# A two-block transformer on one core: conditioning steps spread anew over the feed-forward layers, and projections that end tile by tile

## The chip, the core and the metric

The kernel runs on one core of a Trainium2 chip. The core has a matrix engine (PE, with its weight loads PEld), a vector engine (DVE), a scalar engine (ACT), a general engine (POOL) and a sync engine (SP), which here does nothing but issue loads; 16 DMA engines move the data. The metric is the device time of one execution in microseconds (us).

## What is computed

All is float32. A first block of two layers works on 256 tokens of 1024 features, a second block of four layers on these and on 256 context tokens. What the change touches lies in the first block, and in the conditioning rows `sh`, `sc`, `gt`, which need only `c` and `c_ctx` and can be computed at any time before the second block.

```python
def conv_ffn(h, w_up, ffn_dw_w, ffn_dw_b, w_down):
    u = causal_dwconv(h @ w_up, ffn_dw_w, ffn_dw_b)
    gate, val = jnp.split(u, 2, axis=-1)
    return (jax.nn.silu(gate) * val) @ w_down
...
# first block, each layer l; token_mix ends with "return merged @ w_o"
mix = token_mix(h, positions, w_in[l], ..., w_o[l])
h = layer_norm(DEEPNORM_ALPHA * h + mix, ln1_g[l], ln1_b[l])
ffn = conv_ffn(h, w_up[l], ffn_dw_w[l], ffn_dw_b[l], w_down[l])
h = layer_norm(DEEPNORM_ALPHA * h + ffn, ln2_g[l], ln2_b[l])
...
# second block, each layer i
sh, sc, gt = jnp.split(jax.nn.silu(c) @ ada_w[i] + ada_b[i], 3, axis=-1)
shc, scc, gtc = jnp.split(jax.nn.silu(c_ctx) @ ada_w[i] + ada_b[i], 3, axis=-1)
h = rms_norm(x, norm_g[i]) * (1.0 + sc[:, None]) + sh[:, None]
```

`w_o` is 1024 x 1024, `w_up` 1024 x 5632, `w_down` 2816 x 1024, `ada_w` four times 1024 x 3072.

## The kernel before

**Weights.** All weights lie packed in one array in the order in which they are read (`_plan`), cut into loads of 512 KB. `wload` (L167) issues the next load on SP's queue into a tile `raw` (pool `raw`, 3 buffers, or the side pool `raw2`, 5 buffers). A load waits for the instruction that last read its buffer, and the queue is worked in order. `wsplit` (L177) makes two tiles of a raw one: `whi`, a rounded copy by ACT (L185), and `wlo`, the remainder by DVE (L186). `mm3` (L199) adds three matmuls for each product: hi by lo, hi by hi, lo by hi. `chunk` (L189) loads and splits a whole chunk at high priority: the scheduler, which writes each engine's order, puts it ahead of other work.

**A first-block layer** is `token_mix`, `proj_ln`, `ffn`. `proj_ln` (L731) multiplies by `w_o` in four chunks of 256 columns; each has two token tiles t of 128, and each tile's sum is added to the residual `x[t]` (L744) with statistics per chunk (L745). `layer_norm` (L340) then makes mean and 1/sqrt of each tile (`rsqrt`, some 11 small DVE instructions), scales both halves of 512 features (L352, L353), and `to_feat` (L232) transposes them on PE (L237), copies them on ACT (L238) and subtracts on DVE (L239). The result `hT` is what the next matmuls need.

**The feed-forward part** (`ffn`, L753) takes 22 steps f. Each has an up chunk of 256 columns (two loads, 48 matmuls of 256 columns), a short convolution and gate on ACT and DVE, and, two steps later, the down products of that f: one load of `w_down`, 12 matmuls of 512 columns into four accumulators (`down`). At the end comes the second norm (L811, L812, `layer_norm`).

**Conditioning.** The rows take 96 steps, 48 in each layer. A step (`ada_step`, L277) is one load of 512 KB into `raw2` and four matmuls 32 x 256 (L291, counted in the profile as eight instructions). Eight steps fill one accumulator `ps_o`, which DVE then adds to the bias (L295) and POOL writes to a tensor `adar`. Table `ADA_F` sets five steps ahead of step f = 0, 38 within the feed-forward steps (one or two each) and five behind the last.

**Tiles of pool `big`** (4 buffers, 16 KB in each partition) hold `hT`, the combined branches, the gates and `mT`, the input of `w_o`.

In the words below, "x0" and "x1" are the two token tiles, and T0 is the start of the first up matmul of f = 0.

Of the kernel before, what the change touches and what calls it, by code (L numbers as in the profile page):

```python
# [73 lines left out]
def _plan():  # L74
# [3 lines left out]
    ada = [(i, w, k) for i in range(4) for w in range(3) for k in range(KT)]  # L78
    for l in range(2):
# [16 lines left out]
        for j in range(4):  # L96
            p.chunk("w_o", l, a(256 * j, 256 * j + 256))
# [40 lines left out]
class _Net:  # L138
    def __init__(self, ctx, tc, io, out, dbg):
# [17 lines left out]
        self.load = 0  # L157
        self.ada_acc = None
# [6 lines left out]
    # weights  # L165

    def wload(self, side=False):  # L167
# [3 lines left out]
        t = (self.raw2 if side else self.raw).tile([128, RAWN], F32, name="raw")  # L171
        w = self.io["ws"]
        self.nc.sync.dma_start(t[:, :n], bass.AP(tensor=w.tensor, offset=w.offset + self.off, ap=[[n, 128], [1, n]]))
# [3 lines left out]
    def wsplit(self, src, n, side):  # L177
        nc = self.nc
        pool = self.wsp2 if side else self.wsp
# [9 lines left out]
    def chunk(self, n_k=KT, side=False):  # L189
        """The next chunk: [(hi, lo)] per row tile of 128, each [128, columns]."""  # L190
        out = []
        with self.tc.high_priority() if self.load >= 4 else ExitStack():
            while len(out) < n_k:
                t, k, c = self.wload(side)
                hi, lo = self.wsplit(t, k * c, side)
                out += [(hi[:, b * c:(b + 1) * c], lo[:, b * c:(b + 1) * c]) for b in range(k)]
        return out

# [33 lines left out]
    def to_feat(self, src, hi_dst, lo_dst):  # L232
        """Transposes src [128 tokens, 512] to 4 tiles of features, split in hi and lo."""
# [7 lines left out]
    def qstack(self, ps, n, pool, name="qs", bufs=2):  # L241
        """ps: [two heads x 64, n]; returns [128, head, n] with hi and lo of a head stacked."""
# [8 lines left out]
    def kstack(self, ps, n, hh, ll):  # L251
        """hh: hi of a head on both halves, [128, head, n]; ll: lo on the half of the head, zeros on the other."""
# [8 lines left out]
    def logits(self, out, qs, e, qsl, ks, ksl):  # L261
        """q . k of head e: hi.lo, then (hi + lo).hi."""
# [14 lines left out]
    def ada_step(self):  # L277
        nc = self.nc
        if not self.ada_todo:
            return  # L280
        i, w, k = self.ada_todo.pop(0)
        with self.tc.high_priority():
            t, _, _ = self.wload(True)
# [9 lines left out]
        if k == KT - 1:  # L293
            row = self.w1.tile([128, 256], F32, name="adarow")
            nc.vector.tensor_tensor(row, ps[:, :256], self.ada_b, op=OP.add)  # L295
# [7 lines left out]
    # set-up  # L303

    def setup(self):
# [10 lines left out]
        # the first norm's gains and offsets, spread over the partitions by the tensor engine  # L316
# [44 lines left out]
    def block1(self):  # L361
        nc, tc = self.nc, self.tc
        with ExitStack() as ctx:
# [13 lines left out]
            for l in range(2):  # L377
# [4 lines left out]
                hT = self.proj_ln(l, m)  # L382
                with ExitStack() as c2:
# [4 lines left out]
                    hT = self.ffn(l, hT)  # L388
# [59 lines left out]
    def rope1(self, z, H, t):  # L448
        """In place on z [128, H * 64]."""
# [11 lines left out]
    def token_mix(self, l, hT):  # L461
# [46 lines left out]
        # scores and the chosen keys  # L508
# [32 lines left out]
        # attention over the chosen keys  # L541
# [50 lines left out]
    def conv_in(self, l, hT):  # L592
# [3 lines left out]
        w = self.chunk()  # L596
# [15 lines left out]
        # pooling  # L612
# [8 lines left out]
    def conv_pool(self, l, comb):  # L621
# [27 lines left out]
        # depthwise convolution, its layer norm and silu  # L649
# [609 lines left out]
```

## Time and profile before

| | us |
|---|---|
| median of 3 runs | 2018.33 (2016.28 to 2025.07) |
| span of the profiled execution | 2011.9 |
| PE busy | 1914.8 (95%) |
| DVE busy | 1562.3 (78%) |
| ACT busy | 1011.1 (50%) |
| layer 0: w_o starts, first up matmul, last down matmul | 197.22, 240.12, 449.21 |
| layer 1: w_o starts, first up matmul | 638.13, 678.17 |

The span is from the first to the last instruction; the times of the runs have a little more around it. Busy shares are means over very different stages: in the feed-forward part PE is never idle, while around the norms it stands still several times. A wait is put down to the instruction that released it. A stretch at half the TensorE clock shows as a granted clock below 1.00 in a window's row and as longer matmuls.

### The profile page before, as it was taken

What the parts mean: (1) busy time and instruction counts of PE and PEld (TensorE: products, weight loads), DVE (VectorE), ACT (ScalarE), POOL (GpSimd) and SP (SyncE); (2) the same over time, 40 slices, a digit from 0 to 9 for tenths busy, and PEclk for the clock granted to TensorE, in tenths of its full rate; (3) what the DMA queues carried; (4) which work ended last, traced back from release to release, by engine and by line L of the source; (5) the groups of instructions that cost most, each with busy time, mean ns of one, the idle gap of its engine ahead of it and who ended that gap; (6) DMA issues with size and microseconds to landing.
All of it is one profiled execution on the core that took longest, in us unless ns stands there. A gap on an engine that the chain in (4) does not pass through costs nothing.

```text
span 2011.9 us, 37184 instructions
## 1 busy us (share of the span) xinstructions
PE 1914.8 (95%) x14168; PEld 1692.9 (84%) x14168; DVE 1562.3 (78%) x3881; ACT 1011.1 (50%) x1971; POOL 144.0 (7%) x268
## 2 busy tenths in 40 slices
PE   7999899998999899998999999999998999988898
PEld 6998788888998788877888888988887999978787
DVE  6999676677999768677777587777668888877876
ACT  4564354543564445543565545455453655553564
POOL 2001201001002111011000010000000000000000
PEclk9999899998999899998999999999999999999999
DMA  6444868774445878763111142212224221213321
GB/s 210 170 148 143 296 244 278 265 254 149 150 133 185 292 246 275 266 222 109 43 56 53 53 137 74 82 58 83 77 82 121 68 70 64 66 58 111 105 64 53
DMA packets 82401, 282.31 MB, mean 140 GB/s; under 512 B 12336, under 2 KB 13088, under 8 KB 82224
## 3 DMA queue, kind: packets, MB, share of 16 engines
q1 hardware_dynamic: 70128, 252.04, 37.4%
q0 software_dynamic: 11664, 27.31, 4.7%
q8 instruction: 112, 1.84, 0.4%
q10 hardware_dynamic: 432, 0.59, 0.1%
q14 instruction: 65, 0.53, 0.1%
HBM read 278.75 MB, written 1.15 MB: 139 GB/s over the span
## 4 chain that ended last, share of the span: by engine, by line
PE 33%; issue 15%; DVE 4%; ACT 1%; DMA 1%; POOL 1%; POOLq 0%; ACTq 0%; DVEq 0%
PE acc L201 7%; PE acc L203 7%; PE acc L202 7%; PE ps_o L1068 3%; PE ps_t L1030 2%; PE ps_s L264 2%; PE ps_s L265 1%; PE ps_o L1058 1%; DMA bc<-adar 1%; DVE wlo L186 1%; PE ps_t L965 0%; ACT whi L185 0%; DVE htmp L828 0%; DVE ll L259 0%; DVE hh L257 0%
## 5 line engine op out<-in xcount | busy, mean ns | idle before, releaser
L186 DVE TENSOR_TENSOR wlo<-raw,whi 128x1024 fp32r<-128x1024 f32 (+1 forms) x382 | 465.1, 1223 | 227.6 <-ACT whi L185 213.3
L185 ACT CAST whi<-raw 128x1024 fp32r<-128x1024 f32 (+1 forms) x382 | 398.0, 1046 | 353.7 <-PE acc L202 89.9
L201 PE MATMUL acc<-wlo,big 128*128 128x256 f32 (+2 forms) x1640 | 486.3, 297 | 17.4 <-DVE wlo L186 9.6
L203 PE MATMUL acc<-whi,big 128*128 128x256 f32 (+2 forms) x1640 | 480.4, 294 | 6.9 <-DVE big L239 6.1
L202 PE MATMUL acc<-whi,big 128*128 128x256 f32 (+2 forms) x1640 | 479.4, 293 | 0.0
L201 PEld LDWEIGHTS acc<-wlo,big 128*128 128x128 f32 x1640 | 315.1, 192 | 34.4 <-DVE wlo L186 10.3
L203 PEld LDWEIGHTS acc<-whi,big 128*128 128x128 f32 x1640 | 314.2, 192 | 17.8 <-DVE big L239 8.6
L202 PEld LDWEIGHTS acc<-whi,big 128*128 128x128 f32 x1640 | 315.2, 192 | 8.1 <-issue 3.9
L201 PE MATMUL acc<-big,whi 128*128 128x256 f32 (+1 forms) x864 | 272.2, 315 | 11.6 <-DVE rs_a L221 4.1
L203 PE MATMUL acc<-big,wlo 128*128 128x256 f32 (+1 forms) x864 | 270.5, 314 | 1.0 <-DVE wlo L186 0.9
L202 PE MATMUL acc<-big,whi 128*128 128x256 f32 (+1 forms) x864 | 270.0, 313 | 0.0
L201 PE MATMUL ps_s<-big,whi 128*128 128x256 f32 x704 | 200.2, 284 | 1.0 <-ACT whi L185 0.9
L203 PE MATMUL ps_s<-big,wlo 128*128 128x256 f32 x704 | 199.8, 284 | 0.9 <-DVE wlo L186 0.9
L202 PE MATMUL ps_s<-big,whi 128*128 128x256 f32 x704 | 200.0, 284 | 0.0
L201 PEld LDWEIGHTS acc<-big,whi 128*128 128x128 f32 x864 | 167.4, 194 | 22.1 <-issue 8.7
L203 PEld LDWEIGHTS acc<-big,wlo 128*128 128x128 f32 x864 | 166.6, 193 | 11.0 <-issue 2.1
L202 PEld LDWEIGHTS acc<-big,whi 128*128 128x128 f32 x864 | 167.2, 194 | 8.0 <-issue 1.7
L1023 ACT ACTIVATE p<-ps_s,mx 128x512 f32<-128x512 f32 (+1 forms) x224 | 133.5, 599 | 62.5 <-DVE mx L1015 32.8
L1015 DVE TENSOR_REDUCE mx<-ps_s 128x1 f32<-128x512 f32 (+1 forms) x192 | 105.4, 555 | 48.9 <-PE ps_s L265 43.4
L201 PEld LDWEIGHTS ps_s<-big,whi 128*128 128x128 f32 x704 | 135.6, 193 | 3.9 <-ACT whi L185 1.1
L202 PEld LDWEIGHTS ps_s<-big,whi 128*128 128x128 f32 x704 | 135.7, 193 | 1.6
L203 PEld LDWEIGHTS ps_s<-big,wlo 128*128 128x128 f32 x704 | 135.9, 193 | 1.2 <-DVE wlo L186 1.2
(278 smaller groups left out, 3233.6 us busy)
## 6 DMA issues: line engine op xcount, KB each, us to landing
raw<-in_ws_dram SPq DMA_DIRECT2D x472, 512.0 KB, 4.3
bc<-adar POOLq DMA_DIRECT2D x32, 256.0 KB, 4.4
rpb<-in_rpb_dram POOLq DMA_DIRECT2D x32, 128.0 KB, 2.4
gts<-adar POOLq DMA_DIRECT2D x14, 256.0 KB, 4.2
bc<-in_ln_g_dram POOLq DMA_DIRECT2D x8, 256.0 KB, 6.9
bc<-in_ln_b_dram POOLq DMA_DIRECT2D x8, 256.0 KB, 6.1
raw<-in_ws_dram SPq DMA_DIRECT2D x4, 492.0 KB, 4.3
b_tok<-in_b_tok_dram POOLq DMA_DIRECT2D x10, 164.0 KB, 3.6
```

What stands on the lines that cost most here:

```text
L185: nc.scalar.copy(hi[:, :n], src[:, :n])
L186: nc.vector.tensor_tensor(lo[:, :n], src[:, :n], hi[:, :n].bitcast(F32), op=OP.subtract)
L201: mm(ps, lh, rl, start=start, stop=False)
L202: mm(ps, lh, rh, start=False, stop=False)
L203: mm(ps, ll, rh, start=False, stop=stop)
L264: self.nc.tensor.matmul(out, qs[:, e, qsl], ll[:, e, ksl], start=True, stop=False)
L265: self.nc.tensor.matmul(out, qs[:, e, qsl], hh[:, e, ksl], start=False, stop=True)
L1015: nc.vector.tensor_reduce(mx, sp[:, :n], axis=AX.X, op=OP.max, negate=True)
L1023: nc.scalar.activation(p[:, :n], sp[:, :n], AF.Exp, bias=mx, scale=1.0, accum_out=su)
L1030: nc.tensor.transpose(pt[:, k * 128:k * 128 + 128], p[:, k * 128:k * 128 + 128], self.ident)
L1058: nc.tensor.matmul(po[:, c * 128:c * 128 + 128], pT[:, m, :], vs[k][:, 128 * vp:128 * vp + 128], start=m == 0, stop=m == len(kts) - 1)
L1068: nc.tensor.matmul(po[64 * e:64 * e + 64, c * 128:c * 128 + 128], vs[k][:, 128 * vp + 64 * e:128 * vp + 64 * e + 64], pTs[e][:, m, :], sta ...
```

## The change

Three things change in each first-block layer; bytes, number of steps and arithmetic are the same.

First, `w_o` is read in two chunks of 512 columns. The first is multiplied k by k for both token tiles; the second token tile by token tile, so that x0's sums are complete before x1's begin. The last three down products also run token tile by token tile.

Second, the 48 conditioning steps of a layer are set anew: 12 (layer 0) or 9 (layer 1) ahead of the feed-forward steps, 27 or 29 in the odd steps f alone (two or three in each), and 9 or 10 behind. Those ahead are issued behind the up chunk of f = 0: five go to `raw2`, the others into one or two tiles `big`. Those behind are issued behind the first chunk of what follows, which is now loaded earlier (`w_next`). The up chunk of f = 1 is no longer of high priority.

Third, when a conditioning row is complete, ACT copies it out of `ps_o` before DVE adds the bias.

```diff
+ADA = []
+for _head, _tail in ((12, 9), (9, 10)):
+    _n = 48 - _head - _tail
+    ADA.append([_head, [0 if f % 2 == 0 else _n * (f + 1) // NF - _n * (f - 1) // NF for f in range(NF)], _tail])
...
-        for j in range(4):
-            p.chunk("w_o", l, a(256 * j, 256 * j + 256))
+        for j in range(2):
+            p.chunk("w_o", l, a(512 * j, 512 * j + 512))
...
-        step(ADA_F[-2])
+        head, inner, tail = ADA[l]
         for f in range(NF + 2):
             if f < NF:
                 p.chunk("w_up", l, np.concatenate([a(f * 128, f * 128 + 128), a(FF + f * 128, FF + f * 128 + 128)]))
-                step(ADA_F[f])
+                step(head if f == 0 else 0)
+                step(inner[f])
             if f >= 2:
                 p.chunk("w_down", l, a(D), rows=a((f - 2) * 128, (f - 1) * 128), n_k=1)
-        step(ADA_F[-1])
+        first = len(p.loads)
+        step(tail)
+        tails.append((first, tail))
...
+    for first, n in tails:
+        o = p.loads
+        o[first:first + n + 2] = o[first + n:first + n + 2] + o[first:first + n]
...
+        t = side if isinstance(side, bass.AP) else (self.raw2 if side else self.raw).tile([128, RAWN], F32, name="raw")
...
-    def chunk(self, n_k=KT, side=False):
-        """The next chunk: [(hi, lo)] per row tile of 128, each [128, columns]."""
+    def chunk(self, n_k=KT, side=False, pools=None, urgent=True):
         out = []
-        with self.tc.high_priority() if self.load >= 4 else ExitStack():
+        with self.tc.high_priority() if urgent and self.load >= 4 else ExitStack():
             while len(out) < n_k:
                 t, k, c = self.wload(side)
-                hi, lo = self.wsplit(t, k * c, side)
+                hi, lo = self.wsplit(t, k * c, side, pools.pop(0) if pools else None)
...
+    def ada_steps(self, n, big=0, after=None):
+        steps = self.ada_todo[:n]
+        del self.ada_todo[:n]
+        homes = [True] * n
+        for b in range(big):
+            t = self.big.tile([128, 4, RAWN], F32, name="big")
+            for j in range(4):
+                if 5 + 4 * b + j < n:
+                    homes[5 + 4 * b + j] = t[:, j, :]
+        for home, (i, w, k) in zip(homes, steps):
+            with self.tc.issue_after(after.ins) if after is not None else self.tc.high_priority():
+                t = self.wload(home)[0]
+            self.ada_step(i, w, k, t)
...
+            nc.scalar.copy(row, ps[:, :256])
+            nc.vector.tensor_tensor(row, row, self.ada_b, op=OP.add)
...
-        stats = [self.sm.tile([128, 4, 6], F32, name=f"stats{t}") for t in range(2)]
-        for j in range(4):
-            w = self.chunk()
+        stats = [self.sm.tile([128, 2, 6], F32, name=f"stats{t}") for t in range(2)]
+        for j in range(2):
+            w = self.chunk(pools=[self.wsp, self.wsp, self.wsp, self.wsp2] if j else None)
+            ps = [self.acc.tile([128, 512], F32, name="acc") for t in range(2)]
+            for k, t in [(k, t) for k in range(KT) for t in range(2)] if j == 0 else [(k, t) for t in range(2) for k in range(KT)]:
+                a = mT[:, k, :, t * 128:t * 128 + 128]
+                self.mm3(ps[t], a[:, 0], a[:, 1], w[k][0], w[k][1], k == 0, k == KT - 1)
+            if j == 1:
+                up = self.chunk(pools=[self.wsp2, self.wsp2])
+                last = self.dma
             for t in range(2):
-                ps = self.acc.tile([128, 512], F32, name="acc")[:, :256]
-                for k in range(KT):
-                    a = mT[:, k, :, t * 128:t * 128 + 128]
-                    self.mm3(ps, a[:, 0], a[:, 1], w[k][0], w[k][1], k == 0, k == KT - 1)
-                s = self.x[t][:, 256 * j:256 * j + 256]
-                nc.vector.scalar_tensor_tensor(s, s, ALPHA2, ps, op0=OP.mult, op1=OP.add)
+                s = self.x[t][:, 512 * j:512 * j + 512]
+                nc.vector.scalar_tensor_tensor(s, s, ALPHA2, ps[t], op0=OP.mult, op1=OP.add)
                 nc.vector.bn_stats(stats[t][:, j, :], s)
...
+        self.ada_steps(ADA[l][0], 2 - l, last)
+        return hT, up
...
+                w = self.chunk(urgent=f > 1) if f else up
...
+                self.ada_steps(ADA[l][1][f])
...
+                wd[k] = self.chunk(1, True)[0]
+                if k < NF - 3:
+                    products(k, 0)
+                    products(k, 1)
+        for t in range(2):
+            for k in range(NF - 3, NF):
+                products(k, t)
+        self.w_next = self.chunk()
+        last = self.dma
...
+        self.ada_steps(ADA[l][2], 0, last)
```

**PE, layer 0, from the last `w_o` matmuls to T0.** `x_87` and `x_88` are x0 and x1; `ps_o<-raw,cond` are the matmuls of conditioning steps, four to a step here (the profile counts eight). Before:

```order
L201 MATMUL acc<-wlo,big 128x256
L202 MATMUL acc<-whi,big 128x256
L203 MATMUL acc<-whi,big 128x256
L291 MATMUL ps_o<-raw,cond 32x256 x21
L237 MATMUL ps_s<-ident,x_87 128x128 x8
L291 MATMUL ps_o<-raw,cond 32x256 x7
L237 MATMUL ps_s<-ident,x_88 128x128 x4
L291 MATMUL ps_o<-raw,cond 32x256 x5
L237 MATMUL ps_s<-ident,x_88 128x128 x4
L291 MATMUL ps_o<-raw,cond 32x256 x2
L201 MATMUL ps_s<-big,whi 128x256
```

After:

```order
L219 MATMUL acc<-whi,big 128x512
L220 MATMUL acc<-whi,big 128x512
L318 MATMUL ps_o<-raw,cond 32x256 x16
L254 MATMUL ps_s<-ident,x_87 128x128 x8
L318 MATMUL ps_o<-raw,cond 32x256 x4
L254 MATMUL ps_s<-ident,x_88 128x128 x8
L218 MATMUL ps_s<-big,whi 128x256
L219 MATMUL ps_s<-big,whi 128x256
```

Of the 35 small matmuls ahead of T0 (8.75 steps behind `w_o`, one more stood within it) 20 are left, five steps.

**PE, layer 0, from the down products of f = 0 to the second half of f = 1's up chunk (after).** `acc<-wlo,ff_a` and `ps_t<-...` are down products, `ps_s<-big,...` up matmuls, `ps_o` conditioning.

```order
L318 MATMUL ps_o<-big,cond 32x256 x4
L318 MATMUL ps_o<-raw,cond 32x256 x8
L218 MATMUL acc<-wlo,ff_a 128x512
L219 MATMUL acc<-whi,ff_a 128x512
L220 MATMUL acc<-whi,ff_a 128x512
...
L220 MATMUL ps_t<-whi,ff_a 128x512
L318 MATMUL ps_o<-raw,cond 32x256 x5
L220 MATMUL ps_s<-big,wlo 128x256
...
L318 MATMUL ps_o<-raw,cond 32x256 x31
L218 MATMUL ps_s<-big,whi 128x256
```

The matmuls behind the row `x31` are the first that need the second load of f = 1's up chunk; the 12 ahead of it need the first alone. In the kernel before, f = 0, 1 and 2 ran one behind another there, 144 matmuls with no conditioning step between.

**SP, layer 0, the loads around f = 1 (after).** `big_2735` and `big_2736` are the tiles that take the seven further steps ahead; `raw_2893` and `raw_2899` are the two halves of f = 1's up chunk; `raw_3168` is the down weight of k = 1; the others are conditioning steps and down weights.

```order
L186 DMA raw_3154<-in_ws_dram 128x1024
L186 DMA big_2735<-in_ws_dram 128x1024
L186 DMA raw_3168<-in_ws_dram 128x1024
L186 DMA big_2735<-in_ws_dram 128x1024 x3
L186 DMA big_2736<-in_ws_dram 128x1024
L186 DMA raw_3261<-in_ws_dram 128x1024
L186 DMA big_2736<-in_ws_dram 128x1024 x2
L186 DMA raw_2893<-in_ws_dram 128x1024
L186 DMA raw_3354<-in_ws_dram 128x1024
...
L186 DMA raw_3780<-in_ws_dram 128x1024
L186 DMA raw_2899<-in_ws_dram 128x1024
L186 DMA raw_2980<-in_ws_dram 128x1024
```

Before, the same two halves (`raw_2871`, `raw_2877`) stood here:

```order
L173 DMA raw_2835<-in_ws_dram 128x1024
L173 DMA raw_2847<-in_ws_dram 128x1024
L173 DMA raw_2853<-in_ws_dram 128x1024
L173 DMA raw_2859<-in_ws_dram 128x1024
L173 DMA raw_2865<-in_ws_dram 128x1024
L173 DMA raw_2692<-in_ws_dram 128x1024
L173 DMA raw_2871<-in_ws_dram 128x1024
L173 DMA raw_2877<-in_ws_dram 128x1024
L173 DMA raw_2952<-in_ws_dram 128x1024
```

They stood right behind the five steps ahead and the second half of f = 0 (`raw_2692`); now 20 loads lie from `raw_3168` to `raw_2899`.

## Rows read from the trace of the kernel before

**Rows 1.** Page: the span, and the two groups of the splits (busy us, mean ns).
```profile
span 2011.9 us, 37184 instructions
...
L186 DVE TENSOR_TENSOR wlo<-raw,whi 128x1024 fp32r<-128x1024 f32 (+1 forms) x382 | 465.1, 1223 | 227.6 <-ACT whi L185 213.3
L185 ACT CAST whi<-raw 128x1024 fp32r<-128x1024 f32 (+1 forms) x382 | 398.0, 1046 | 353.7 <-PE acc L202 89.9
```

**Rows 2.** Busy time of two stretches: PE, PEld, DVE, ACT, POOL, granted clock, DMA share, GB/s.
```profile
203.50:240.00 36.50, 28.60 (x231) 23.05 (x229) 24.32 (x58) 9.42 (x11) 8.13 (x16) 0.86 0.84 296
240.00:447.00 207.00, 207.00 (x1578) 181.94 (x1577) 145.99 (x233) 107.99 (x156) 21.60 (x44) 1.00 0.77 268
```

**Rows 3.** Waits of PE, whole run: who for whom, us in total, times, longest.
```profile
PE ps_s L237 <- DVE x L353: 9.7, 3, 6.1
```

**Rows 4.** PE in time order, layer 0: start us, us, line, instruction, [idle before, releaser].
```profile
197.22 0.36 PE L201 MATMUL acc<-wlo,big 128*128 128x256 f32 x1 [0.72 <-DVE wlo L186]
...
220.62 0.57 PE L201 MATMUL acc<-wlo,big 128*128 128x256 f32 x1 [3.03 <-DVE wlo L186]
...
225.18 2.37 PE L291 MATMUL ps_o<-raw,cond 128*32 128x256 f32 x40
232.41 1.06 PE L291 MATMUL ps_o<-raw,cond 128*32 128x256 f32 x2 [4.86 <-DMA raw<-in_ws_dram]
...
240.12 0.39 PE L201 MATMUL ps_s<-big,whi 128*128 128x256 f32 x1
240.34 0.28 PE L202 MATMUL ps_s<-big,whi 128*128 128x256 f32 x1
240.46 0.28 PE L203 MATMUL ps_s<-big,wlo 128*128 128x256 f32 x1
```

**Rows 5.** DVE grouped, norm behind layer 0's feed-forward part (447.6 to 464.8): busy us, mean ns.
```profile
L352 DVE SCALAR_TENSOR_TENSOR x<-x,mv,bc 128x512 f32<-128x512 f32 x4 | 3.0, 743 | 0.0
...
L239 DVE TENSOR_TENSOR big<-ps_s,big 128x512 fp32r<-128x512 f32 x4 | 2.7, 687 | 1.1 <-ACT big L238 1.1
L812 DVE BATCH_NORM_STATS2 stats<-x 128x6 f32<-128x512 f32 x4 | 2.6, 679 | 0.0
...
L219 DVE SCALAR_TENSOR_TENSOR rs_a<-rs_y,rs_v 128x1 f32<-128x1 f32 x6 | 1.2, 205 | 0.1
```

**Rows 6.** The same columns as Rows 2, two stretches of 5 us.
```profile
210.00:215.00 5.00, 5.00 (x44) 5.00 (x43) 2.77 (x6) 0.00 (x0) 0.00 (x0) 1.00 1.03 355
...
230.00:235.00 5.00, 2.60 (x10) 1.75 (x10) 4.89 (x19) 0.45 (x1) 1.46 (x3) 0.59 1.02 407
```

**Rows 7.** Tile `raw`, 203 to 262 us: its loads (count, first and last start) and landing.
```profile
L173 SPq DMA_DIRECT2D raw<-in_ws_dram x31: 327/328/808, 203.7 to 259.9; - x31
...
DMA to landing us min/median/max: 3.2/6.5/11.5
```

**Rows 8.** PE grouped, conditioning matmuls within layer 0's feed-forward part.
```profile
L291 PE MATMUL ps_o<-raw,cond 128*32 128x256 f32 x272 | 20.0, 387 | 0.0
```

**Rows 9.** PE in time order, the end of layer 0's feed-forward part.
```profile
448.98 0.39 PE L202 MATMUL ps_t<-whi,ff_a 128*128 128x512 f32 x1
449.21 0.39 PE L203 MATMUL ps_t<-whi,ff_a 128*128 128x512 f32 x1
449.53 2.37 PE L291 MATMUL ps_o<-raw,cond 128*32 128x256 f32 x40
...
463.53 0.58 PE L201 MATMUL acc<-big,whi 128*128 128x256 f32 x1
```

**Rows 10.** PE in time order, layer 1.
```profile
638.13 0.36 PE L201 MATMUL acc<-wlo,big 128*128 128x256 f32 x1 [0.72 <-DVE wlo L186]
...
665.45 2.49 PE L291 MATMUL ps_o<-raw,cond 128*32 128x256 f32 x40
...
678.17 0.38 PE L201 MATMUL ps_s<-big,whi 128*128 128x256 f32 x1
...
910.95 1.97 PE L237 MATMUL ps_s<-ident,htmp 128*128 128x128 f32 x8 [9.06 <-DVE htmp L828]
```

More of the change, by code (lines that the diff above doesn't have):

```diff
@@ L78, in _plan @@
     ada = [(i, w, k) for i in range(4) for w in range(3) for k in range(KT)]
+    tails = []
     for l in range(2):
@@ L157, in __init__ @@
         self.load = 0
+        self.w_next = None
         self.ada_acc = None
@@ L170, in wload, with wsplit @@
         n = len(rows) // 128 * len(cols)
-        t = (self.raw2 if side else self.raw).tile([128, RAWN], F32, name="raw")
+        t = side if isinstance(side, bass.AP) else (self.raw2 if side else self.raw).tile([128, RAWN], F32, name="raw")
         w = self.io["ws"]
-        self.nc.sync.dma_start(t[:, :n], bass.AP(tensor=w.tensor, offset=w.offset + self.off, ap=[[n, 128], [1, n]]))
+        self.dma = self.nc.sync.dma_start(t[:, :n], bass.AP(tensor=w.tensor, offset=w.offset + self.off, ap=[[n, 128], [1, n]]))
         self.off += 128 * n
         return t, len(rows) // 128, len(cols)
-    def wsplit(self, src, n, side):
+    def wsplit(self, src, n, side, pool=None):
         nc = self.nc
-        pool = self.wsp2 if side else self.wsp
+        pool = pool or (self.wsp2 if side else self.wsp)
         if self.wsp3 is not None:
@@ L187, in wsplit, with next_chunk @@
         return hi, lo
-    def chunk(self, n_k=KT, side=False):
+    def chunk(self, n_k=KT, side=False, pools=None, urgent=True):
         out = []
-        with self.tc.high_priority() if self.load >= 4 else ExitStack():
+        with self.tc.high_priority() if urgent and self.load >= 4 else ExitStack():
             while len(out) < n_k:
                 t, k, c = self.wload(side)
-                hi, lo = self.wsplit(t, k * c, side)
+                hi, lo = self.wsplit(t, k * c, side, pools.pop(0) if pools else None)
                 out += [(hi[:, b * c:(b + 1) * c], lo[:, b * c:(b + 1) * c]) for b in range(k)]
         return out
+    def next_chunk(self):
+        w, self.w_next = self.w_next, None
+        return w or self.chunk()
     def mm3(self, ps, lh, ll, rh, rl, start, stop):
@@ L275, in row_tile, with ada_step @@
         return t
-    def ada_step(self):
-        nc = self.nc
[L279 to L283, printed above, removed]
+    def ada_steps(self, n, big=0, after=None):
[11 more added lines that the diff above has]
+            self.ada_step(i, w, k, t)
+    def ada_step(self, i, w, k, t):
+        nc = self.nc
         if k == 0:
@@ L294, in ada_step @@
             row = self.w1.tile([128, 256], F32, name="adarow")
-            nc.vector.tensor_tensor(row, ps[:, :256], self.ada_b, op=OP.add)
+            nc.scalar.copy(row, ps[:, :256])
+            nc.vector.tensor_tensor(row, row, self.ada_b, op=OP.add)
             if w == 1:
@@ L381, in block1 @@
                     m = self.token_mix(l, hT)
-                hT = self.proj_ln(l, m)
                 with ExitStack() as c2:
@@ L758, in ffn, with products @@
                 nc.gpsimd.dma_start(self.x[2 + t], self.io["ctx_2"][t * 128:t * 128 + 128, :])
-        acts = {}
+        acts, wd = {}, {}
         down = [[self.acc.tile([128, 512], F32, name="acc") for _ in range(2)],
                 [self.acc.tile([128, 512], F32, name="acc"), self.psT.tile([128, 512], F32, name="ps_t")]]
-        for _ in range(ADA_F[-2]):
-            self.ada_step()
+        def products(k, t):
+            at = acts[k]
+            for h in range(2):
+                sl = slice(512 * h, 512 * h + 512)
+                self.mm3(down[t][h], at[:, 0, t * 128:t * 128 + 128], at[:, 1, t * 128:t * 128 + 128],
+                         wd[k][0][:, sl], wd[k][1][:, sl], k == 0, k == NF - 1)
         for f in range(NF + 2):
             if f < NF:
-                w = self.chunk()
+                w = self.chunk(urgent=f > 1) if f else up
                 ps = self.psS.tile([128, 2, S], F32, name="ps_s")
@@ L785, in ffn @@
                 acts[f] = at
-                for _ in range(ADA_F[f]):
-                    self.ada_step()
+                self.ada_steps(ADA[l][1][f])
                 if l == 0 and f == 8:
@@ L794, in ffn @@
                 k = f - 2
-                w = self.chunk(1, True)
-                at = acts.pop(k)
-                for t in range(2):
-                    for h in range(2):
-                        sl = slice(512 * h, 512 * h + 512)
-                        self.mm3(down[t][h], at[:, 0, t * 128:t * 128 + 128], at[:, 1, t * 128:t * 128 + 128],
-                                 w[0][0][:, sl], w[0][1][:, sl], k == 0, k == NF - 1)
-        for _ in range(ADA_F[-1]):
-            self.ada_step()
+                wd[k] = self.chunk(1, True)[0]
[7 more added lines that the diff above has]
+        last = self.dma
         self.lng = [self.bcast(self.io["ln2_g"], 512, D * l + 512 * h) for h in range(2)]
@@ L981, in v_chunk @@
     def v_chunk(self, order=range(4)):
-        w = self.chunk()
+        w = self.next_chunk()
         vs = {}
```

8 lines of the change are left out of this document (3 added, 5 removed).

## Prediction

> **What bounds the kernel now.** The windows by stage come first: in layer 0's feed-forward part PE is busy 207.00 of 207.00 us, while around the first norm it is busy 28.60 of 36.50 and its granted clock is 0.86 [rows 2]. So a step taken out of the feed-forward part is worth its PE time, and one put into an idle stretch is free if its weights are there. PE's waits then say what the idle stretches wait for: among them the scaling of the norm on DVE, 9.7 us [rows 3]. The PE timeline places another kind: `w_o` runs from 197.22 to 225.18 with a hole of 3.03 us before its last chunk, five steps take 2.37 us, then PE idles 4.86 us for the next load, and the first up matmul starts at 240.12 [rows 4]. The last view is the loads: 31 start between 203.7 and 259.9, one every 1.87 us, and land after 6.5 us in the median [rows 7]. DMA moves 355 to 407 GB/s where it is not held up [rows 6]. This front is held by two things at once, the norm on DVE and the loads; the change frees the first and asks more of the second.
>
> **The change, part by part, layer 0.**
>
> *w_o in 512 columns.* Before: 28.0 us [rows 4]. After: 96 matmuls of 512 columns at 0.23 us (448.98 to 449.21) [rows 9], 22.1 us, so the end is at 219.3. The hole of 3.03 us waited for a split whose load shared the queue with conditioning loads; these now stand behind. If it comes back the end is at 222.3.
>
> *Start of the up matmuls (T0).* The last 24 matmuls are x1's alone, so x0's sums are there at 213.8. From then on DVE has, for each tile, an add and a statistics instruction of 0.68 (the row of the statistics stands for both), four scalings of 0.74, and some 11 small ones (1/sqrt: six take 1.2 us for two tiles, all together about 1.9 a tile) [rows 5]: 6.3 us, twice 12.6. Add three subtractions of 0.69 [rows 5] and two splits of 1.22 [rows 1] (f = 0's second half, and the first down weight, which DVE's order has ahead of the last two subtractions): 17.1 us. T0 is 230.9 against 240.12, a gain of 9.2; ends 6 (the hole is back) and 11.6 (both splits done before 213.8). I take 9.
>
> *Steps.* Before T0 stood 9.75 steps (8.75 behind `w_o`, by PE's order), now five. So the PE-bound part has 48 - 5 - 9 = 34 steps instead of 48 - 9.75 - 5 = 33.25: the larger head does not unload it, since only five of the twelve have a place ahead of T0. A step there costs 20.0 / 34 = 0.59 us [rows 8], one in a run 2.37 / 5 = 0.47 [rows 4]. Some 18 now come in runs: 0.75 x 0.59 - 18 x 0.12 = -1.7.
>
> *The loads behind the steps ahead.* This is the term that decides. On SP the seven loads into `big`, the down weights and the loads of twelve inner steps stand ahead of f = 1's second half. The load of the second down weight (`raw_3168`) waits for the split of the first, which stands in DVE's order behind x1's norm, about 229.5. Behind it, in the same queue, come 20 loads, the last of them f = 1's second half (`raw_2899`). The trace has no such train; the nearest rows give three rates. 512 KB take 1.29 us at 407 GB/s, 1.48 at 355 [rows 6], 1.87 at the mean of the 31 loads [rows 7]. With 3.2 us, the shortest landing [rows 7], for the last one and 1.05 + 1.22 for cast and split [rows 1], f = 1 can go on at 260.8, 264.6 or 272.4. PE has until then: 48 up matmuls at 0.12 [rows 4], 18 steps at 0.47, 12 down products at 0.23, 12 matmuls on f = 1's first half: 5.8 + 8.5 + 2.8 + 1.4 = 18.5, to 249.4. Stall: 11, 15 or 23 us. I take 15, the rate of the stretch in which the queue had most to do and least to wait for. Before, these two loads stood right behind the five steps ahead, and PE had no wait there.
>
> The Trainium skill, "DMA: Bandwidth & Descriptors", section Specifications, puts the HBM limit of a core at about 358 GB/s; by it the train could not be quicker than 1.46 us a load and the stall not under 15. The row of 407 GB/s [rows 6] stands against it as a hard limit, so the end at 11 stays.
>
> *Clock.* After an idle of 3.03 us the matmuls are twice as long, 0.57 in the record [rows 4], and 230 to 235 shows a mean of 0.59 of the 2.4 GHz [rows 6]. The stall will be followed by such a stretch: 0 to 3 us, less what goes in the front. I take +1. The Trainium skill, "TensorE: Matmul & The Clock Gate", section "Why this matters for your kernels", asks for no PE-idle gap over about 3 us; by it each piece of the stall would cost the clock anew, while the work in between is hidden by the stall anyway, so only what follows counts.
>
> *End of the part.* x0's last sum now lies 18 down products before the end instead of 6: 12 x 0.23 = 2.8 us earlier. The two splits of the next chunk, now loaded early, put 2.4 us back on DVE, which bounds the stretch of 14 us from the last product to the next stage's first matmul at 463.53 [rows 9]. The row's copy on ACT costs nothing: ACT waits in this stretch. -0.4, ends -2.8 and +1.
>
> Layer 0: -9 - 1.7 + 15 + 1 - 0.4 = **+4.9 us**, from about -4 to +17.
>
> **Layer 1.** `w_o` takes 27.3 us (638.13 to 665.45) [rows 10], after 22.1; by the same sum T0 is 671.8 against 678.17: -6.4. Steps, by the same count in PE's order: 9.25 ahead before, five now, 33 within the bound part against 33.75; some ten come in runs: -1.6. The train is short here: one tile `big`, and both halves of f = 1 stand right behind it, five loads behind the one that waits for x1's norm (670.4): ready at 670.4 + 5 x 1.48 + 3.2 + 2.3 = 683.3, with PE's work reaching to 681 or 684. f = 2's second half is nine loads further, 696.6, with work to 694.4. So 0 to 6 us, +2 taken, net of short waits that were there before. At the end the conditioned norm's 9.06 us of idle [rows 10] take five more steps without getting longer (2.4 us of work), and x0 is earlier as above: -0.6. Layer 1: **-6.6 us**, from -10 to 0.
>
> Nothing else in the kernel moves: the second block has the same loads and order.
>
> **Sum.** -1.7 us. The profiled execution has a span of 2011.9 [rows 1]; the median of the runs, 2018.33, lies 6.4 above the span, and I add the sum to that: 2016.6, **2016**. A measurement of this kernel can tell about 0.5%, 10 us, from no change, so this is a forecast of no change that can be told: the front's gain is given back by the queue.
>
> **Rivals.**
>
> *The queue keeps up (faster).* Both fronts are shorter and the loads don't hold PE long: the train goes at 407 GB/s or better, and its first wait ends before 229.5, because the first down weight's split slips into a hole of DVE. Then the stall is 2 instead of 15 and the clock's 1 us is not lost: -1.7 - 14 = -16, 2002. For it: 407 GB/s was reached for 5 us [rows 6]. Against: the order of DVE is fixed, and from 203.7 on the mean was 1.87 us a load.
>
> *Hops instead of a train (slower).* Eleven of the 20 loads wait for a conditioning step that frees their buffer, and that step waits for a load itself. If each such turn takes a landing of 6.5 us [rows 7] and not a place in the train, three turns and their steps behind the last load into `big` (about 243) lead to 243 + 3 x 7 + 6.5 + 2.3 = 273, a stall of 23; in layer 1 the same turn behind f = 1 makes 8 instead of 2, and the clock costs 3 more in all: -1.7 + 8 + 6 + 3 = +15, 2034. It decides from a landing of about 5 us a turn. For it: landings of up to 11.5 us in this stretch. Against: the shortest was 3.2.
>
> *The front gains only w_o's matmuls (the change doesn't do what it says).* DVE stays in the same order of work, urgent splits stand between the small instructions of 1/sqrt, and T0 comes 5 and 3 us earlier instead of 9 and 6: +7, 2024. For it: before, too, DVE was hardly idle in the norm: 4.89 us of 5 [rows 6].
>
> **How the numbers follow.** Forecast 0.40; the queue keeps up 0.27; hops 0.20; only w_o 0.13. Of the forecast a little reaches beyond either bound (0.03 each), of the hops a fifth stays within it. Faster 0.28, same 0.53, slower 0.19. For 8 in 10 the range must reach both rivals: 2000 to 2034. The likeliest case alone, with its bounds, is 2007 to 2028.
>
> **What would show it.** Right: `w_o` of 22 us and T0 near 231 and 672; a wait of PE for a split or a load between T0 and f = 2, 15 us in layer 0, a few in layer 1; SP's queue waiting for PE's conditioning matmuls in that stretch; a shorter end of the feed-forward part by nothing or little. Wrong: up matmuls of f = 0, 1 and 2 without a hole between them (then 2002), a hole of over 20 us or one of over 6 in layer 1 (2034), T0 after 235 (2024).

## The result, and the profile after

The changed kernel takes 2034.64 us (2032.9 to 2035.9, 4 runs) against 2018.13 before: a ratio of 1.0075, interval 1.0052 to 1.0098. It is slower by 16 us, where no change was forecast. The span of its profiled execution is 2031.4, 19.5 more than before [rows 1].

The windows by stage of the changed kernel, with the columns of [rows 2]: `w_o` to T0, the feed-forward part and its end in layer 0, then the first two of these in layer 1.

```profile
198.00:231.60 33.60, 27.59 (x149) 20.22 (x149) 30.49 (x58) 11.91 (x16) 9.32 (x14) 0.97 0.83 283
231.60:464.60 233.00, 217.38 (x1596) 188.48 (x1600) 150.08 (x240) 109.74 (x160) 19.67 (x39) 0.95 0.71 242
464.60:480.20 15.60, 9.09 (x89) 4.54 (x84) 12.80 (x39) 2.78 (x6) 9.13 (x19) 0.85 0.62 202
653.20:686.60 33.40, 28.11 (x149) 20.94 (x150) 31.15 (x70) 13.36 (x20) 9.31 (x14) 0.95 0.85 271
686.60:910.40 223.80, 215.94 (x1604) 188.87 (x1608) 157.87 (x258) 112.06 (x166) 20.17 (x40) 0.98 0.75 253
```

The same stages of the kernel before:

```profile
197.20:240.10 42.90, 34.58 (x272) 28.45 (x272) 30.14 (x66) 11.28 (x14) 10.28 (x19) 0.88 0.81 284
240.10:449.60 209.50, 209.50 (x1592) 183.84 (x1594) 148.00 (x237) 107.89 (x156) 21.50 (x43) 1.00 0.76 267
449.60:463.50 13.90, 6.46 (x56) 4.12 (x56) 13.21 (x41) 1.77 (x4) 8.35 (x17) 0.74 0.38 82
638.10:678.20 40.10, 33.24 (x269) 27.83 (x269) 30.73 (x75) 12.85 (x18) 9.23 (x17) 0.91 0.84 285
678.20:893.70 215.50, 213.53 (x1611) 186.68 (x1614) 156.90 (x258) 110.80 (x163) 23.16 (x46) 0.99 0.77 265
```

Both fronts are shorter, by 9.3 and 6.7 us. Layer 0's feed-forward part is longer by 23.4: PE, never idle there before, stands still for 15.6 us and is busy 7.9 us longer, at a mean granted clock of 0.95 instead of 1.00. Layer 1's is longer by 8.3.

| stretch | forecast | measured |
|---|---|---|
| layer 0: `w_o` to T0 | -9 | -9.3 |
| layer 0: feed-forward part (steps, loads, clock) | +14.3 | +23.4 |
| layer 0: end of the part | -0.4 | +1.7 |
| layer 0 to 1: start of `w_o`, attention | 0 | -0.7 |
| layer 1: `w_o` to T0 | -6.4 | -6.7 |
| layer 1: feed-forward part | +0.4 | +8.3 |
| layer 1: end, up to the first q and k transposes | -0.6 | -0.3 |
| the rest | 0 | +3.3 |

The last line is not put down to the change: from those transposes to the last matmul's end, the eleven kernels profiled here take 1062.7 to 1068.1 us with the same code there, and the longer ones spend more of it at the lower clock (see the last section).

The PE timeline after T0 shows the hole (start, us, line, instruction, [idle before, releaser]):

```profile
231.63 0.58 PE L218 MATMUL ps_s<-big,whi 128*128 128x256 f32 x1 [0.56 <-DVE big L256]
...
246.39 0.56 PE L218 MATMUL acc<-wlo,ff_a 128*128 128x512 f32 x1 [3.26 <-ACT ff_a L820]
...
263.49 0.88 PE L318 MATMUL ps_o<-raw,cond 128*32 128x256 f32 x8 [5.00 <-DMA raw<-in_ws_dram]
...
270.27 1.08 PE L318 MATMUL ps_o<-raw,cond 128*32 128x256 f32 x8 [4.40 <-DMA raw<-in_ws_dram]
...
273.92 0.58 PE L218 MATMUL ps_s<-big,whi 128*128 128x256 f32 x1 [1.29 <-ACT whi L198]
...
275.18 0.58 PE L220 MATMUL ps_s<-big,wlo 128*128 128x256 f32 x1 [0.46 <-DVE wlo L199]
```

PE waits 3.26 us for f = 0's gate, then for step loads, 5.00 and 4.40 us, and at 273.92 for the cast of f = 1's second half: a chunk that it could have worked on from 249.4, by the forecast's count of the work at hand. The waits of SP's queue from 231 to 267, in which f = 1's second half gets its turn (us in total, times, longest):

```profile
SPq L186 <- PE ps_o L318: 10.2, 6, 3.7
SPq L186 <- DVE wlo L199: 8.9, 3, 4.1
SPq L186 <- DMA raw<-in_ws_dram: 7.8, 3, 3.4
SPq L186 <- DVE ff_a L821: 2.7, 1, 2.7
```

What the engines did until that half had landed, as a window with the columns of [rows 2]:

```profile
231.00:273.00 42.00, 27.25 (x217) 15.37 (x216) 10.38 (x16) 7.52 (x12) 10.02 (x20) 0.78 0.86 310
```

The landing of the loads into `raw` issued there:

```profile
DMA to landing us min/median/max: 3.2/5.8/8.8
```

SP waits for buffers most of this time, yet the DMA engines behind it are busy to 0.86 and move 310 GB/s; a load takes 5.8 us in the median. The train of 20 loads runs from 231.00 to 266.31, one every 1.77 us. What the missing 0.14 is, stands below under the step that failed.

### The profile page after: what moved, and what is told of

Its sections match the earlier page's. It is cut to its first block, busy times and chain, and to the rows that moved or that the text cites. A ratio compares the mean times of both kernels' runs of the same rounds, so it can differ in the third digit from the quotient of the medians.

```text
span 2031.4 us, 36806 instructions
## 1 busy us (share of the span) xinstructions
PE 1921.5 (95%) x13976; PEld 1688.9 (83%) x13976; DVE 1562.5 (77%) x3865; ACT 1016.3 (50%) x1983; POOL 144.2 (7%) x268
## 4 chain that ended last, share of the span: by engine, by line
PE 62%; issue 16%; DVE 13%; DMA 5%; ACT 3%; POOL 1%; DVEq 0%; SPq 0%; POOLq 0%; ACTq 0%
PE acc L218 12%; PE acc L220 11%; PE acc L219 11%; PE ps_s L220 4%; PE ps_s L218 4%; PE ps_s L219 4%; DVE wlo L199 4%; DMA raw<-in_ws_dram 3%; PE ps_o L1105 3%; PE ps_s L281 2%; PE ps_t L1067 2%; PE ps_s L282 2%; PE ps_o L318 1%; ACT whi L198 1%; PE ps_o L1095 1%
## 5 line engine op out<-in xcount | busy, mean ns | idle before, releaser
L218 PE MATMUL acc<-wlo,big 128*128 128x256 f32 (+2 forms) x1576 | 476.3, 302 | 14.0 <-ACT big L255 3.7
L220 PE MATMUL acc<-whi,big 128*128 128x256 f32 (+2 forms) x1576 | 470.6, 299 | 6.1 <-DVE big L256 6.1
L219 PE MATMUL acc<-whi,big 128*128 128x256 f32 (+2 forms) x1576 | 469.7, 298 | 0.0
L218 PEld LDWEIGHTS acc<-wlo,big 128*128 128x128 f32 x1576 | 303.7, 193 | 34.6 <-ACT big L255 7.7
L220 PEld LDWEIGHTS acc<-whi,big 128*128 128x128 f32 x1576 | 303.7, 193 | 19.2 <-DVE big L256 8.4
L219 PEld LDWEIGHTS acc<-whi,big 128*128 128x128 f32 x1576 | 303.9, 193 | 10.9 <-issue 4.4
L218 PE MATMUL ps_s<-big,whi 128*128 128x256 f32 x704 | 203.7, 289 | 6.8 <-ACT whi L198 5.4
L219 PE MATMUL ps_s<-big,whi 128*128 128x256 f32 x704 | 202.3, 287 | 0.0
L218 PEld LDWEIGHTS ps_s<-big,whi 128*128 128x128 f32 x704 | 138.2, 196 | 13.2 <-ACT whi L198 8.3
L219 PEld LDWEIGHTS ps_s<-big,whi 128*128 128x128 f32 x704 | 138.2, 196 | 2.2 <-issue 0.8
```

Of the source, the lines that this page charges most:

```text
L218: mm(ps, lh, rl, start=start, stop=False)
L219: mm(ps, lh, rh, start=False, stop=False)
L220: mm(ps, ll, rh, start=False, stop=stop)
```

## The experiments

**One edit: the priority of f = 1's chunk.** The theory after the result: the loss is that chunk's place in the queue, which its missing priority makes.

```diff
-                w = self.chunk(urgent=f > 1) if f else up
+                w = self.chunk() if f else up
```

> The changed kernel with one edit: the up chunk of f = 1 is of high priority again, as all others. In SP's order both halves of f = 1 then stand right behind those of f = 0, ahead of the steps. Theory (the chunk's place behind a train of loads that wait for conditioning steps makes the loss of 24 us in layer 0's feed-forward part and part of the 8 us in layer 1): 2010 to 2018 us, no idle of PE for f = 1 in layer 0. Rival (twelve steps ahead ask too much of the DMA engines, in whatever order): the wait moves to the steps or to f = 2, 2025 to 2035 us.

Measured: 2012.82 us, 0.9971 (0.9955 to 0.9987). One word gives 22 us back: the feed-forward parts take 209.7 and 213.2 us, as before the change, and no wait for f = 1 is left. But T0 comes 16.8 and 18.6 us behind the end of `w_o`, where the changed kernel takes 11.7 and 11.4. The PE timeline of this kernel tells why:

```profile
222.32 0.64 PE L318 MATMUL ps_o<-raw,cond 128*32 128x256 f32 x8 [1.24 <-DMA raw<-in_ws_dram]
230.67 1.06 PE L318 MATMUL ps_o<-raw,cond 128*32 128x256 f32 x2 [7.71 <-DMA raw<-in_ws_dram]
...
237.85 0.38 PE L218 MATMUL ps_s<-big,whi 128*128 128x256 f32 x1 [0.40 <-DVE big L256]
```

Up loads now stand ahead of the steps' loads, and PE has the steps ahead of the transposes: it waits 7.71 us for a step that nobody needs yet.

**Fewer steps ahead, no tiles `big`, the priority as changed.**

```diff
-for _head, _tail in ((12, 9), (9, 10)):
+for _head, _tail in ((5, 9), (5, 10)):
...
-        self.ada_steps(ADA[l][0], 2 - l, last)
+        self.ada_steps(ADA[l][0], 0, last)
```

> The changed kernel with five steps ahead in both layers instead of 12 and 9 (none in tiles big), the others moved into the odd steps f (34 and 33 there); f = 1's up chunk stays without priority. Rival (the seven loads into big are what holds the queue): the stall goes, 2012 to 2018 us. Theory (the place of f = 1's chunk behind loads that wait for steps): its second half still stands some 17 loads behind f = 0, most of them waiting for steps, so the stall stays at 15 to 25 us and the time at 2028 to 2038 us.

Measured: 2034.24 us, 1.0072 (1.0049 to 1.0096), with parts of 227.1 and 230.4 us. The seven loads into `big` are not needed for the loss: without them other step loads stand ahead of f = 1.

**The old step counts, without and with the priority.** Both have 5 steps ahead, 38 within, 5 behind, and no tile `big`; the second has the priority as well (the last two lines of the edit) and writes the same counts in the loop.

```diff
-ADA = []
-for _head, _tail in ((12, 9), (9, 10)):
...
+ADA = [[5, [38 * (f + 1) // NF - 38 * f // NF for f in range(NF)], 5] for _ in range(2)]
...
-        self.ada_steps(ADA[l][0], 2 - l, last)
+        self.ada_steps(ADA[l][0], 0, last)
...
-                w = self.chunk(urgent=f > 1) if f else up
+                w = self.chunk() if f else up
```

> The changed kernel with the step counts of before (5 ahead, one or two in every f, 5 behind, no tiles big), f = 1's up chunk still without priority: the twin of e8_old_counts_urgent, which differs in that priority alone. Theory (a chunk without priority is put behind every step load that has it, here some 20): the stall of 15 to 25 us in each layer's first steps is there, 2035 to 2055 us. Rival (steps bunched in odd f or the steps in big make the stall): none of either is here, so as e8, 2015 to 2021 us.

> The changed kernel with the step counts of before (5 ahead, 38 within at one or two in each f, 5 behind, none in tiles big) and f = 1's up chunk of high priority: what is left is w_o in 512 columns, sums tile by tile, the early loads of the next chunk, the copy on ACT. Theory (these parts gain in both fronts, the steps' new places lose): 2000 to 2008 us, T0 near 232 in layer 0. Rival (the projections' part gains nothing without the steps moved behind urgent loads): 2014 to 2020 us.

Measured without: 2045.57 us, 1.0133 (1.0105 to 1.0161), the slowest of all, with the step counts of the kernel before. With the priority: 2018.01 us, 0.9989 (0.9975 to 1.0003). So the priority is worth 28 us here, and that was foreseen; that the rest would gain was not borne out (2000 to 2008 was expected, with T0 near 232; T0 is 235.63). Its T0 comes 15.5 and 19.0 us behind `w_o`, for the reason of e1_urgent: waits of 6.50 and 7.17 us for a step's load. The order of the loads counts twice: f = 1 too late costs in the feed-forward part, the steps too late cost ahead of T0, because PE's order has them there.

**The inner steps spread over all f.**

```diff
-... [0 if f % 2 == 0 else _n * (f + 1) // NF - _n * (f - 1) // NF for f in range(NF)] ...
+... [_n * (f + 1) // NF - _n * f // NF for f in range(NF)] ...
```

> The changed kernel with its 27 and 29 inner steps spread over all f (one or two each) instead of two or three in the odd ones; the steps ahead, behind, and f = 1's missing priority stay. In SP's order both halves of f = 1 then stand 8 loads nearer. Theory (place in the queue counts): the stall shrinks by 8 places at 1.3 to 1.8 us, to about 10 us in layer 0, 2016 to 2026 us. Rival (it is the demand of the steps ahead as such): unchanged, 2030 to 2036 us.

Measured: 2022.04 us, 1.0017 (1.0005 to 1.0028), the parts 223.2 and 218.4 us. Bringing the chunk nearer brings part of the time back. Bunching is a part of the loss as far as it puts loads ahead of that chunk or, in layer 1, ahead of the chunks behind it: f = 1 stands at the same 17 places there in both kernels (table below), and the part is 5.4 us shorter.

**Places and time.** Counting in SP's order the places from f = 0's last load to f = 1's last, and reading each part's length from the PE timelines:

| kernel | layer 0: places, part (us) | layer 1: places, part (us) | median |
|---|---|---|---|
| e1_urgent | 2, 209.7 | 3, 213.2 | 2012.82 |
| e8_old_counts_urgent | 2, 212.7 | 3, 218.5 | 2018.01 |
| e3_wo_only (below) | 2, 211.7 | 2, 216.6 | 2009.83 |
| before | 3, 209.5 | 3, 215.5 | 2018.13 |
| e9_f1_behind5 (below) | 12, 210.2 | 12, 215.1 | 2006.70 |
| e11_f1_behind5_tail5 (below) | 12, 212.7 | 12, 215.4 | 2006.33 |
| e15_nobig (below) | 16, 212.4 | 16, 214.6 | 2010.59 |
| changed | 32, 232.9 | 17, 223.8 | 2034.64 |
| e4_even | 21, 223.2 | 17, 218.4 | 2022.04 |
| e5_head5 | 28, 227.1 | 28, 230.4 | 2034.24 |
| e2_oldsteps | 31, 232.4 | 31, 238.1 | 2045.57 |

Up to 16 places the part is within some 3 us of the kernel before, with 2 places as with 16; the parts hold 30.5 to 39.5 conditioning steps, against some 34 before, at some 0.6 us each. At 17 the table has 218.4 and 223.8 us, at 21 the part is longer by 13.7, and at 28 to 32 by 15 to 23 us. So the part grows with the place of f = 1, but the place is not the whole price. In the kernels with 12 places and more, f = 1's last load lands 1.55 to 1.84 us a place behind f = 0's last. The same stretch, 203 to 273 us, as a window of four kernels, with the columns of [rows 2]. The changed kernel:

```profile
203.00:273.00 70.00, 49.77 (x345) 31.48 (x343) 35.29 (x67) 17.04 (x23) 17.27 (x33) 0.86 0.87 308
```

e1_urgent:

```profile
203.00:273.00 70.00, 59.15 (x418) 46.14 (x420) 50.29 (x91) 28.76 (x40) 11.72 (x21) 0.93 0.85 294
```

e2_oldsteps:

```profile
203.00:273.00 70.00, 49.48 (x343) 31.46 (x341) 36.52 (x69) 17.05 (x23) 17.74 (x33) 0.84 0.88 306
```

e9_f1_behind5:

```profile
203.00:273.00 70.00, 62.53 (x452) 50.46 (x451) 53.53 (x97) 29.52 (x42) 13.05 (x24) 0.95 0.87 311
```

294 to 311 GB/s in all four, with DMA shares of 0.85 to 0.88, while PE's busy time differs between 49.48 and 62.53 of 70 us. The engines move about as much in the good order as in the bad one; what differs is whose bytes come first.

**w_o alone, in the kernel before.**

```diff
-        for j in range(4):
-            p.chunk("w_o", l, a(256 * j, 256 * j + 256))
+        for j in range(2):
+            p.chunk("w_o", l, a(512 * j, 512 * j + 512))
...
+            ps = [self.acc.tile([128, 512], F32, name="acc") for t in range(2)]
+            for k, t in [(k, t) for k in range(KT) for t in range(2)]:
...
```

> The kernel before with w_o alone changed: two chunks of 512 columns, k by k for both token tiles, statistics in two parts; steps, their loads and all else as before. Theory (the front's gain of 9 and 7 us, measured in the changed kernel, comes from w_o, and is kept if the loads are not rearranged): 4 to 6 us a layer from the matmuls, 2006 to 2011 us. Rival (the front waits for conditioning loads, 4.86 us before, so shorter matmuls only lengthen that wait): 2014 to 2019 us.

Measured: 2009.83 us, 0.9948 (0.9933 to 0.9963). This piece alone is worth about 9 us by the medians, and 7 to 14 by the interval. In its profiled execution the way from the start of `w_o` to T0 takes 37.1 and 38.2 us instead of 42.9 and 40.0: of the 4 to 6 us a layer that were expected layer 1 keeps 1.9.

**The chunk of f = 1 behind the first five steps.** It has the priority, but stands behind five step loads; the other steps ahead, in `big`, stand behind it.

```diff
-        self.ada_steps(ADA[l][0], 2 - l, last)
-        return hT, up
+        self.ada_steps(5, 0, last)
+        with self.tc.issue_after(self.dma.ins):
+            up1 = self.chunk()
+        self.ada_steps(ADA[l][0] - 5, NBIG[l], self.dma)
+        return hT, (up, up1)
...
```

The rest of the edit puts the plan of the loads and the tiles `big` into the same order.

> The changed kernel with f = 1's up chunk of high priority but held behind the first five step loads, the other steps ahead (7 and 4, in tiles big) behind it; step counts as changed. Theory (e1_urgent lost 6 and 7 us ahead of T0 because its five steps' loads came behind nine up loads): T0 again about 11.7 us behind the end of w_o in both layers, no stall for f = 1, 1998 to 2006 us. Rival (the loads of the steps and of f = 1 can't both be in time, one of them makes PE wait): 2009 to 2016 us.

Measured: 2006.70 us, 0.9942 (0.9922 to 0.9961), faster than both kernels, though just above the 1998 to 2006 expected. T0 lies 12.4 and 14.6 us behind `w_o`, the parts take 210.2 and 215.1 us: the hole is gone and the front is kept, in layer 1 with 3 us less than hoped. There PE waits 3.78 us for the norm on DVE and 1.67 for its last subtraction; why DVE is later was not tested.

**Five steps behind layer 0's part instead of nine.** The end of the part had grown by 1.7 us in the changed kernel. In e9_f1_behind5 the PE timeline there reads:

```profile
447.46 0.64 PE L321 MATMUL ps_o<-raw,cond 128*32 128x256 f32 x8 [0.92 <-DMA raw<-in_ws_dram]
450.83 0.64 PE L321 MATMUL ps_o<-raw,cond 128*32 128x256 f32 x8 [2.73 <-DMA raw<-in_ws_dram]
...
457.90 1.67 PE L257 MATMUL ps_s<-ident,x 128*128 128x128 f32 x8 [2.49 <-DVE x L384]
459.93 0.58 PE L221 MATMUL acc<-big,whi 128*128 128x256 f32 x1 [0.36 <-DVE big L259]
```

```diff
-for _head, _tail in ((12, 9), (9, 10)):
+for _head, _tail in ((12, 5), (9, 10)):
```

> As e9_f1_behind5, with five steps behind layer 0's feed-forward part instead of nine (31 within instead of 27). The changed kernel's end of that part took 15.6 us against 13.9 before, with PE waiting for loads of steps that stand ahead of the first transposes. Theory (these waits lengthen the end): the end takes 12.5 to 14 us, the feed-forward part 2 us more, the whole within 2 us of e9. Rival (DVE's norm sets the end, with nine steps as with five): the end stays at 15 to 16 us and the time rises by 2 us.

The same view of this kernel:

```profile
445.24 2.37 PE L321 MATMUL ps_o<-raw,cond 128*32 128x256 f32 x40
451.46 1.78 PE L257 MATMUL ps_s<-ident,x 128*128 128x128 f32 x8 [3.85 <-DVE x L384]
...
458.62 0.58 PE L221 MATMUL acc<-big,whi 128*128 128x256 f32 x1 [0.55 <-DVE big L259]
```

Measured: 2006.33 us, 0.9943 (0.9921 to 0.9966). The five steps run without a wait, the end takes 13.3 us instead of 16.4, and the part takes 2.4 us more: no difference in sum. Nine steps there were not free: their loads come too late and hold the transposes that stand behind them on PE.

**Are the early loads into `big` worth anything?** As the last kernel, with five steps ahead in both layers and none in `big`:

```diff
-for _head, _tail in ((12, 5), (9, 10)):
+for _head, _tail in ((5, 5), (5, 10)):
...
-NBIG = (2, 1)
+NBIG = (0, 0)
```

> As e11_f1_behind5_tail5, but with five steps ahead in both layers and none in tiles big: the 7 and 4 others go into the odd steps f (38 and 33 there), f = 1's up chunk stays of high priority behind the first five steps' loads. Theory (the steps in big are done on PE behind T0 in any case, so their place gains nothing; what gains is w_o, and f = 1's chunk being in time): within 4 us of e11, 2002 to 2010 us. Rival (steps loaded early into unused tiles relieve the loads of the feed-forward part): 2011 to 2018 us, with PE waiting for loads in the steps f = 1 to 8.

Measured: 2010.59 us, 0.9964 (0.9947 to 0.998). It lies between the two expectations and its interval overlaps that of the kernel with `big` (0.9921 to 0.9966): some 4 us by the medians, not settled. In the profiled executions the parts are no longer than with `big` (212.4 and 214.6 against 212.7 and 215.4). With `w_o` alone at 0.9948, nothing here shows that the moved steps are worth a measurable time by themselves.

## Why the prediction was wrong

*Right.* The fronts: T0 at 231.63 where 230.9 was worked out, gains of 9.3 and 6.7 for 9 and 6.4. So was the reading that both `w_o`'s matmuls and the norm on DVE set it; ahead of T0 PE waits for the norm:

```profile
223.43 1.32 PE L254 MATMUL ps_s<-ident,x 128*128 128x128 f32 x8 [1.34 <-DVE x L381]
...
229.33 1.75 PE L254 MATMUL ps_s<-ident,x 128*128 128x128 f32 x8 [4.01 <-DVE x L381]
```

That ACT's copy of a row is free no run shows: PE waits for it four times in the whole run, 1.6 us in sum, 0.49 of it at the end of layer 0's part. The sign and place of the counter-effect were right too: a hole ahead of f = 1's second half in layer 0, seen from SP's order alone.

*The step that failed* is the size of "The loads behind the steps ahead": a stall of 15 us was taken, and it is 23.8. (By the forecast's count PE has work for 18.5 us from T0, here to 250.1, and goes on at 273.92.) The sum had a train without a gap at 1.48 us a load, "the rate of the stretch in which the queue had most to do and least to wait for", and the shortest landing, 3.2 us. PE goes on 9.3 us later than its 264.6, for four reasons. The train's first load is issued at 231.00 instead of 229.5: +1.5. That load takes 6.1 us to land and not 3.2 (231.00 to 237.10): +2.9. From there 20 loads land in 35.7 us, the last at 272.80, 1.785 us each: +6.1. And PE needs the cast alone to go on, not cast and split: -1.2.

The 35.7 us can be divided. The DMA engines work 29.0 of them on these 20 loads, 1.45 us each, so the forecast's rate was that of the busy engines; 1.5 us go to the small loads of POOL's queue, and for 5.1 us the engines are idle. Of the idle 3.5 us fall into the 12 us in which only one or two loads are on the way while SP waits for a buffer. The windows of 5 us show it (columns as in [rows 2]): DMA shares of 0.95 to 1.02 where the queue is full, 0.63 to 0.73 where it runs thin.

```profile
235.00:240.00 5.00, 5.00 (x41) 3.51 (x41) 0.00 (x0) 1.03 (x1) 0.00 (x0) 0.86 1.02 412
240.00:245.00 5.00, 3.07 (x35) 1.67 (x33) 3.49 (x7) 1.93 (x6) 2.24 (x5) 1.00 0.73 273
...
250.00:255.00 5.00, 5.00 (x47) 2.93 (x47) 1.22 (x1) 1.02 (x1) 0.00 (x0) 0.99 0.63 220
255.00:260.00 5.00, 3.00 (x38) 1.56 (x37) 2.08 (x3) 1.42 (x2) 2.32 (x5) 1.00 0.73 247
...
265.00:270.00 5.00, 0.87 (x8) 0.00 (x0) 0.00 (x0) 0.00 (x0) 0.50 (x1) 0.50 0.98 316
270.00:275.00 5.00, 2.96 (x18) 0.91 (x18) 1.10 (x1) 1.97 (x2) 0.00 (x0) 0.50 0.95 347
```

So a window of 5 us with a full queue was taken for a rate that had to hold for 35, in which the queue was not always full. The rows had nearer numbers: [rows 2] has 296 GB/s for the front as a whole, its idle included, which is 1.77 us for 512 KB, and [rows 7] a median landing of 6.5. With these the forecast's sum gives 229.5 + 35.4 + 6.5 + 2.3 = 273.7; that it meets 273.92 so closely is in part luck, since the later start and the split that PE need not wait for cancel.

The Trainium skill, "DMA: Bandwidth & Descriptors", section Specifications, puts a core's HBM limit at about 358 GB/s. No stretch of 40 us or more that was read here came nearer to it than 324 (e4_even, 231 to 273, DMA share 0.90), which agrees; a window of 5 us reached 412, so there it is no limit.

*In layer 1* the same term: five places at 1.48 were reckoned, and the last of them took 10.4 us to land (689.05 to 699.43). PE waits only 1.0 us for f = 1 there, but 4.5 us more for the splits of the chunks behind it, up to 736.95, which are late as well. Over the part PE is idle 7.9 us instead of 2.0 and busy 2.4 longer, which makes the 8.3 against +0.4. e1_urgent has 213.2 us there; e4_even, with the same 17 places and its inner steps spread, has 218.4, so the bunched steps behind f = 1 have a share in it.

*The clock* was put at +1. After the idles of 5.00 and 4.40 us the eight matmuls of a step take 0.88 and 1.08 us for what took 0.62 to 0.64, and the stretch from 265 to 270 has a granted clock of 0.50, the lower level of 1.2 GHz. The clock falls three times from 229 to 264 us, each time behind a longer idle of PE (4.01, 3.26 and 5.00 us). That agrees with the Trainium skill, "TensorE: Matmul & The Clock Gate", section "Why this matters for your kernels", which warns of idle gaps above about 3 us between bursts. Layer 0's part has 25.3 us at the lower level, against none before. 18.4 of them lie ahead of 273.92, where the loads set the end; the 6.9 behind it cost some 3.5 us (an estimate: half of them).

*The end of layer 0's part* was to gain 0.4 and lost 1.7: the step that failed is that nine steps behind it cost nothing. Their loads, issued behind the next chunk, were late, and PE's order has seven of the nine ahead of x0's transposes; it waits 0.94 and 2.26 us for two of them.

*The rivals.* "Hops instead of a train" gave 2034 and a stall of 23, and the time is 2034.6, just above the range, and the stall 23.8. That both numbers fit is in part luck. Its cause has a part in it: most of the 5.1 us of idle engines in the train comes with SP's waits, and the loads issued at 257.68, 264.40 and 271.41 each wait for the step of a load before, 6.7 and 7.0 us apart, the turn that it priced. But its price was one landing a turn and not places in a train, and at the end each such turn carries four loads, with the engines busy to 0.92 and more from 260 us on. In the seven kernels with 12 to 32 places the price of a place stays at 1.55 to 1.84 us, while SP waits 10.2 us for steps in the changed kernel and 19.2 in e2_oldsteps (231 to 267 us). So most of it is the train; what more buffers for the steps would give back was not tried. "The queue keeps up" falls with the stall. "The front gains only `w_o`'s matmuls" falls with T0 at 231.63.

*Two readings put right.* In the kernel before, `raw_2692` is the last load of `w_o`, and `raw_2871` and `raw_2877` are the halves of f = 0; those of f = 1 are `raw_2952` and `raw_2958`, one and three places behind. What the forecast used, that f = 1 stood close behind f = 0 and PE had no wait there, holds. And by the prediction's own shares the chances are 0.30 for faster and 0.51 for the same, not 0.28 and 0.53, which changes neither the forecast nor the range.

## What to carry to other kernels

Where DMA is the limit of a stretch, price a load by its place: the sustained rate of that whole stretch with its idle turns, times the places ahead of it on its queue, plus the landing under load, and not the rate of the best few microseconds. Taking the priority from one load puts it behind everything that still has it, so look up where its last piece lands in the queue before anything else about the change. Filler work belongs behind urgent loads in the queue and behind urgent work on its engine, both at once: with the first alone PE waits for the filler.

## What the runs showed of the hardware

The 16 engines' rate from 203 to 273 us was 282 GB/s in the kernel before and 290 to 314 in the other ten, for very different orders and waits, with DMA shares of 0.80 to 0.90. Divided by the share, all eleven come to some 345 to 361 GB/s, so what differs is mostly how long the engines are idle. Windows of 5 us differ more at a full share: 316 GB/s at 0.98 and 412 at 1.02 in the changed kernel.

The program's part behind the first block, the same code in all kernels, takes 1062.7 to 1068.1 us in the eleven profiled executions. The four shortest (up to 1064.4) have 13.7 us of it at the lower clock of 1.2 GHz, the five longest (from 1066.4) 20.5 to 23.9. The same shows from run to run of one kernel: e1_urgent took 2005.92 us at a mean granted clock of 0.986 and 2017.92 at 0.980. What lowers the clock in one execution and not in the next is open.
